# Low halves of the weights: a negated copy on ScalarE and an adding DMA instead of a VectorE subtraction

## The chip, the cores and the metric

One core of one Trainium2 chip runs the whole program. The metric is the device time of one execution in microseconds, as the median of the runs. What a measurement of this kernel can tell from no change is about 0.2%, some 3.5 us.

## The reference, cut to what matters

A two-layer trunk over L = 528 positions (16 learned meta tokens and 512 frames) of width 2048, in float32:

```
h = rms_norm(x); q, k, v, gate = split(h @ a_w_in, 4)          # 2048 x 8192
o = diff_attention(rope(q), rope(k), v)                        # 8 heads, two softmaxes each
x = x + (rms_norm(o, subln) * 0.8 * silu(gate)) @ a_w_out      # 2048 x 2048
k_sh, v_sh = split(rms_norm(x) @ w_kv, 2)                      # 2048 x 512
q, gate = split(rms_norm(x) @ b_w_in, 2)                       # 2048 x 4096
x = x + (window_attention(rope(q), k_sh, v_sh, sinks) * silu(gate)) @ b_w_out
return rms_norm(x)[:, 16:]
```

Nearly all of the arithmetic is in the five weight products, 132 tiles of 128 output features in all.

## The kernel before, in words

Everything is kept transposed: features on the 128 partitions, tokens along the free dimension. TensorE multiplies in a reduced float32 form (F32R), so each operand is split in two: a high half that is the value rounded to that form, and a low half that is the rest. A product is then three matrix products: high by high, high by low, low by high.

`proj(m, hi, lo, cols)` makes the feature tile m: 16 k tiles, three products each, over 528 tokens in two column groups of 264 (FULL, layer A and the shared K/V) or over 512 tokens in one group (REAL, layer B). It asks `wunit(m, half)` twice for a unit of weights, eight k tiles or 128 x 1024 words (512 KB). So a FULL unit is 48 matmuls and a REAL unit 24, and `proj` uses a unit's low half first in the third product of its first k tile.

`wunit` is where the change is. For each unit SyncE (SP) issues the load of the raw words (L98), ScalarE (ACT) copies them into the high half `whi` (L99), and VectorE (DVE) subtracts the high half from the raw words into the low half `wlo` (L100):

```
nc.sync.dma_start(raw[:, c], w[m, half, :, c])
act.activation(hi[:, c], raw[:, c], AF.Copy)
dve.tensor_tensor(out=lo[:, c], in0=raw[:, c], in1=f(hi[:, c]), op=ALU.subtract)
```

There are two places for raw words and three each for `whi` and `wlo`, so the preparing of a unit begins when TensorE has done with the unit three before it. The last four units of the kernel go to places of their own (`place`, the tiles `wu`), and the first two feature tiles are loaded between the pieces of x. That leaves 132 x 2 = 264 units, of which 260 use the three rotating places.

The framework's scheduler orders each engine's instructions when the program is built; what `wunit` issues is put in with raised priority. At run time each engine, and each queue that issues DMAs, takes its instructions strictly in that order. Attention is written as generators whose steps `proj` takes between its k tiles (`advance`).

The stages, in order: the six feature tiles of each of 8 heads with the attention of the head before (until about 670 us), 16 gate tiles (to 870, beside the last head's attention until 740), the output product of layer A with residual, h1 store and sums of squares (870 to 1058), the shared K/V (to 1106), 32 tiles of queries and gates of layer B with its attention (to 1540), the output product of layer B (to 1707), and the last norm.

GpSimd (POOL) has few tasks before: the turned quarter of the rope product (L298, L596), the gated product of layer A (L499), the running sums of squares (L164) and a part of the last norm (L832). It issues no DMA. `norm_b` (L549 and `rms`, L174) waits for the last sum of squares and puts four matmuls into the K/V product.

Of the kernel before, what the change touches and what calls it, by code (L numbers as in the profile page):

```python
# [10 lines left out]
AF = mybir.ActivationFunctionType  # L11
ALU = mybir.AluOpType
# [5 lines left out]
L = SEQ + META  # L18
# [9 lines left out]


class Quads:  # L30
    """Places for [128, 4, 528] words; a freed place is given out again oldest first."""

    def __init__(self, pool, prefix, n):
        self.pool, self.idle, self.n = pool, [f"{prefix}{i}" for i in range(n)], 0
# [9 lines left out]
def trunk(tc, xT, w, vecs, sinks, rope, ident_in, out):  # L44
# [18 lines left out]
    def f(ap):  # L63
        return ap.bitcast(F32)

# [1 line left out]
    ident = cst.tile([128, 128], F32, name="ident")  # L67
    vec = cst.tile([128, 70], F32, name="vec")
    snk = cst.tile([128, 16], F32, name="snk")
# [9 lines left out]
    lam = cst.tile([128, 1], F32, name="lam")  # L79
    subg = cst.tile([128, 2], F32, name="subg")  # L80

# [1 line left out]
    ready = {}  # L83

    def wunit(m, half, place=None, pieces=1, urgent=True):
        """hi and lo of eight k tiles of the weights of feature tile m."""
        if (m, half) in ready:
            return ready.pop((m, half))
        with tc.high_priority() if urgent else ExitStack():
            raw = wp.tile([128, 1024], F32, tag="raw", name="raw", bufs=2)  # L90
            if place is None:
                hi = wp.tile([128, 1024], F32R, tag="whi", name="whi")
                lo = wp.tile([128, 1024], F32R, tag="wlo", name="wlo")
            else:
                hi, lo = place[:, 0, :], place[:, 1, :]
            for i in range(pieces):
                c = slice(1024 // pieces * i, 1024 // pieces * (i + 1))
                nc.sync.dma_start(raw[:, c], w[m, half, :, c])  # L98
                act.activation(hi[:, c], raw[:, c], AF.Copy)  # L99
                dve.tensor_tensor(out=lo[:, c], in0=raw[:, c], in1=f(hi[:, c]), op=ALU.subtract)  # L100
        return hi, lo

    def advance():
        """One step of the work that waits its turn between the halves of a projection."""
        while steps:
            try:
                next(steps[0])
                return True
            except StopIteration:
                steps.popleft()  # L110
        return False
# [32 lines left out]
        return tp.tile([128, L], F32, tag="t", name=name)[:, 0:n]  # L144

    def split4(src, g, hi, lo):
        """hi + lo = src * g, exactly."""
        act.activation(hi, src, AF.Copy, scale=g)
        dve.scalar_tensor_tensor(out=lo, in0=src, scalar=g, in1=f(hi), op0=ALU.mult, op1=ALU.subtract)  # L149

# [13 lines left out]
                pl.tensor_tensor(out=self.acc[i], in0=self.acc[i], in1=t, op=ALU.add)  # L164

    def rms(parts, dst, spare):
        """dst = 1 / sqrt(mean + eps), the same in every partition; parts add up to the sums of squares."""
        n = dst.shape[1]
        ss = psS.tile([128, 2, 512], F32, tag="S", name="ss")
        k = 2 if n > 512 else 1  # L170
        step = n // k
        for s in range(k):
            for i, p in enumerate(parts):
                pe.matmul(  # L174
                    ss[:, s, 0:step], lhsT=ones, rhs=p[:, s * step : s * step + step], start=(i == 0), stop=(i == len(parts) - 1)
                )
        v = (lambda x: two(x)) if k == 2 else (lambda x: x)
        sv = ss[:, :, 0:step] if k == 2 else ss[:, 0, 0:step]
        act.activation(v(dst), sv, AF.Sqrt, bias=epst, scale=1.0 / D)
        dve.reciprocal(out=dst, in_=dst)  # L180
        a, b = spare
        dve.tensor_scalar(out=v(a), in0=sv, scalar1=1.0 / D, scalar2=EPS, op0=ALU.mult, op1=ALU.add)
        dve.tensor_tensor(out=b, in0=dst, in1=dst, op=ALU.mult)
        dve.scalar_tensor_tensor(out=a, in0=a, scalar=-0.5, in1=b, op0=ALU.mult, op1=ALU.mult)
        dve.scalar_tensor_tensor(out=dst, in0=a, scalar=1.5, in1=dst, op0=ALU.add, op1=ALU.mult)
# [13 lines left out]

    sq2 = pool("sq2", 1)  # L200

    # ================= layer A =================
    pA = ExitStack()
    ap = pA.enter_context(tc.tile_pool(name="ap", bufs=1))

# [14 lines left out]
        if q4 % 2 == 1:  # L220
            pl.tensor_tensor(out=xq[q4 - 1], in0=xq[q4 - 1], in1=xq[q4], op=ALU.add)

    # x and the first two feature tiles' weights in the order in which the products take them
    def x_in(*kts):
        for kt in kts:
            nc.sync.dma_start(xq[kt // 4][:, kt % 4, :], xT[kt])
# [25 lines left out]
        Y.free(*xqt)  # L252
        yield

    # lambda, and the gain of the heads' norm with its factors
    lp = sm.tile([128, 2], F32, name="lp", bufs=1)
    dve.tensor_tensor(out=lp[:, 0:1], in0=vec[:, G_LAM : G_LAM + 1], in1=vec[:, G_LAM + 1 : G_LAM + 2], op=ALU.mult)
    dve.tensor_tensor(out=lp[:, 1:2], in0=vec[:, G_LAM + 2 : G_LAM + 3], in1=vec[:, G_LAM + 3 : G_LAM + 4], op=ALU.mult)
# [62 lines left out]
        yield  # L321

    def scores(S, qh, ql, m, q0, n, nsplit):
        """S = q k^T for 128 rows from q0 and n keys."""
        step = n // nsplit
        for s in range(nsplit):
            k0 = s * step
            o = S[:, s, 0:step] if nsplit > 1 else S[:, m, 0:n]
            ks = slice(k0, k0 + step)
            qs = slice(q0, q0 + 128)  # L330
            pe.matmul(o, lhsT=qh[:, m, qs], rhs=qh[:, 2 + m, ks], start=True, stop=False)  # L331
            pe.matmul(o, lhsT=qh[:, m, qs], rhs=ql[:, 2 + m, ks], start=False, stop=False)  # L332
            pe.matmul(o, lhsT=ql[:, m, qs], rhs=qh[:, 2 + m, ks], start=False, stop=True)  # L333

    def combine(p, s, n):
        """p[0] = p[0] / s[0] - lambda p[1] / s[1]"""
        dve.reciprocal(out=s, in_=s)
        dve.tensor_tensor(out=s[:, 1:2], in0=s[:, 1:2], in1=lam[0:n], op=ALU.mult)
        dve.tensor_scalar(out=p[1], in0=p[1], scalar1=s[:, 1:2], scalar2=None, op0=ALU.mult)
        dve.scalar_tensor_tensor(out=p[0], in0=p[0], scalar=s[:, 0:1], in1=p[1], op0=ALU.mult, op1=ALU.subtract)  # L340

    def heads_attend(h, qh, ql, vq, vmh, qktags, vtag):
# [23 lines left out]
        def srows(i):  # L366
            n, q0 = META + 128 * (i + 1), META + 128 * i
            p = [ap.tile([128, L], F32, tag=f"p{m}", name=f"p{m}", bufs=2 - m)[:, 0:n] for m in range(2)]
            nm = sm.tile([128, 2], F32, tag="nm", name="nm")
            s = sm.tile([128, 2], F32, tag="s", name="s")  # L370
            if i < 3:
                S = psS.tile([128, 2, 512], F32, tag="S", name="S")
                for m in range(2):
                    scores(S, qh, ql, m, q0, n, 1)
                # the first chunk's rows see nothing of the second chunk's keys
                dve.memset(S[0:64, :, n - 64 : n], NEG)
                dve.tensor_reduce(out=nm, in_=S[:, :, 0:n], axis=AX.X, op=ALU.max, negate=True)
                for m in range(2):
                    act.activation(p[m], S[:, m, 0:n], AF.Exp, bias=nm[:, m : m + 1], accum_out=s[:, m : m + 1])
            else:  # L380
                for m in range(2):
                    S = psS.tile([128, 2, 512], F32, tag="S", name="S")
                    scores(S, qh, ql, m, q0, n, 2)
                    dve.memset(S[0:64, 1, HALF - 64 : HALF], NEG)
                    dve.tensor_reduce(out=nm[:, m : m + 1], in_=S[:, :, 0:HALF], axis=AX.XY, op=ALU.max, negate=True)
                    act.activation(two(p[m]), S[:, :, 0:HALF], AF.Exp, bias=nm[:, m : m + 1], accum_out=s[:, m : m + 1])
                    if m == 0:
                        yield
            combine(p, s, 128)
            wt[i] = p[0]  # L390
# [62 lines left out]
        tmeta(1)  # L453
        yield
        pv(1)
        # norm over the head's 256 features
        sq = [sq2.tile([128, L], F32, tag=t, name=t) for t in ("sq", "ss1")]
        for dt in range(2):
            act.activation(sq[dt], o[:, dt, :], AF.Square)
# [23 lines left out]
        steps.append(heads_attend(h, *args))  # L483

    def gate_tile(acc, r, o, scale, n, dst=None):
        """o = 2 scale silu(gate) o, or dst = 2 scale silu(gate)"""
        z, th = tmp("z", n), tmp("th", n)
        av = acc[:, :, 0:HALF] if n == L else acc[:, 0, :]
        v = two if n == L else (lambda x: x)
# [9 lines left out]
            pl.tensor_tensor(out=o, in0=z, in1=o, op=ALU.mult)  # L499

    def split_quad(src, P, name, n):
        """hi and lo of a place of four tiles, each in a place of its own."""
        a, ta = P.get([128, 4, L], F32R, f"{name}h")
        b, tb = P.get([128, 4, L], F32R, f"{name}l")
        for k in range(4):
# [30 lines left out]
    drain()  # L536
    pA.close()

    # ================= layer B =================
    pB = ExitStack()  # L540
    bp = pB.enter_context(tc.tile_pool(name="bp", bufs=1))
    swap = [(j + 8) % 16 if j < 16 else j for j in range(32)]
# [162 lines left out]
    held, done, at = {}, [0], [0]  # L705

    def gate_b(m):
        """The gate's product with o in o's place; held back where o is still to come."""
        g = m // 4
        acc = proj(T_GATE_B + m, hh, hl, REAL)  # L710
        if done[0] > g:
# [42 lines left out]
    m = 0  # L754
# [29 lines left out]
    for m in range(KT - LAST):  # L784
# [5 lines left out]
        act.activation(dst, dst, AF.Copy, scale=vec[:, G_F + m : G_F + m + 1])  # L790
        if m == 1:
            act.activation(warm, ss.acc[0][:, 0:1], AF.Sqrt)
    # the last tiles one half of the tokens after the other, so that the first half's end overlaps
    units, rest = [], []
    for i in range(2 * LAST):
        m, half = KT - LAST + i // 2, i % 2
# [42 lines left out]


def _rope_table(rot, period, n_rows):
    """cos and signed sin, [2, 128, L]: rows below rot of every period rows turn, the others stay."""
    inv = np.float32(THETA) ** (-np.arange(0, rot, 2, dtype=np.float32) / np.float32(rot))
    ang = np.arange(L, dtype=np.float32)[None, :] * inv[:, None].astype(np.float32)
    c, s = np.cos(ang).astype(np.float32), np.sin(ang).astype(np.float32)
# [6 lines left out]


def _tiles(wm, cols):
    """Weight columns in tiles of 128: [tile, half, 128, 8 * 128]."""
    t = wm.reshape(2, 8, 128, -1, 128).transpose(3, 0, 2, 1, 4)
    return t[cols].reshape(len(cols), 2, 128, 1024)

# [39 lines left out]
```

## Time and profile before

| | |
|---|---|
| Median of 3 runs | 1748.77 us (1748.36 to 1749.06) |
| Span of the profiled execution, first to last instruction | 1746.9 us |
| TensorE (PE) busy | 1723.8 us, 99% |
| VectorE (DVE) busy | 978.9 us, 56% |
| ScalarE (ACT) busy | 685.8 us, 39% |
| GpSimd (POOL) busy | 170.3 us, 10% |
| DMA | 167.02 MB, mean 96 GB/s |

The profile gives the profiled execution by its span; the median stands 1.9 us above it, for what lies around the first and last instruction. Busy times are those of instructions that compute; those that issue DMAs or wait are not counted. Matmuls are pipelined, so the duration of one (0.29 us for 264 columns) is longer than the distance from one to the next (0.12 us).

### The profile page before, as it was taken

To read this page: it belongs to the slowest core of one execution; us is meant where nothing else is said; L and a number is where in the kernel's file an instruction comes from. 1 tells how busy PE (TensorE), PEld (TensorE's weight loads), DVE (VectorE), ACT (ScalarE), POOL (GpSimd) and SP (SyncE) were. 2 spreads that over 40 slices of the span, in tenths; PEclk is the share of its full clock that TensorE was granted. 3 is DMA by queue.
4 is the path that set the end of the run, shared out by engine and by line. 5 is a ranking of instruction groups with operands and counts; after the bars stand their busy time and mean duration, and the time that the engine had idled before them with its cause. 6 is when DMAs were issued, how large, how long until landed. Compare 5 with 4: busy or idle time off the path is not lost.

```text
span 1746.9 us, 28756 instructions
## 1 busy us (share of the span) xinstructions
PE 1723.8 (99%) x12078; PEld 1608.9 (92%) x12078; DVE 978.9 (56%) x1533; ACT 685.8 (39%) x1261; POOL 170.3 (10%) x106
## 2 busy tenths in 40 slices
PE   8999999999999999999999999999999999999996
PEld 7999999999999999999999999888888788888886
DVE  7755555565656565543333337567677877662234
ACT  6333333343333343433223234344445554553331
POOL 2110101010101010011101110011010100001111
PEclk9999999999999999999999999999999999999998
DMA  6222222222222222222343434422222222233342
GB/s 211 97 80 78 73 73 77 81 74 84 74 74 73 86 73 76 71 93 90 97 148 134 145 129 154 133 85 73 73 72 85 72 73 73 69 110 118 121 127 97
DMA packets 55185, 167.02 MB, mean 96 GB/s; under 512 B 6032, under 2 KB 10256, under 8 KB 55056
## 3 DMA queue, kind: packets, MB, share of 16 engines
q1 hardware_dynamic: 43728, 146.04, 25.6%
q10 hardware_dynamic: 11328, 19.14, 3.3%
q8 instruction: 95, 1.56, 0.4%
q14 instruction: 34, 0.28, 0.1%
HBM read 156.64 MB, written 8.52 MB: 95 GB/s over the span
## 4 chain that ended last, share of the span: by engine, by line
PE 93%; DVE 2%; ACT 1%; POOL 0%; issue 0%; DVEq 0%; ACTq 0%; POOLq 0%
PE acc L126 81%; PE po L424 2%; PE poB L694 2%; PE TB L198 1%; PE acct L813 1%; PE SB L646 1%; PE SB L645 1%; PE S L331 1%; PE S L333 1%; PE S L332 1%; PE T L198 1%; PE Tv L198 0%; DVE wlo L100 0%; PE po L425 0%; DVE h L832 0%; PE Tm L198 0%
## 5 line engine op out<-in xcount | busy, mean ns | idle before, releaser
L99 ACT ACTIVATE whi<-raw 128x1024 fp32r<-128x1024 f32 (+1 forms) x262 | 276.1, 1054 | 620.3 <-PE acc L126 555.2
L100 DVE TENSOR_TENSOR wlo<-raw,whi 128x1024 fp32r<-128x1024 f32 (+1 forms) x262 | 325.9, 1244 | 244.7 <-ACT whi L99 239.2
L126 PE MATMUL acc<-xh,whi 128*128 128x264 f32 x2048 | 424.2, 288 | 3.5 <-ACT whi L99 2.1
L126 PE MATMUL acc<-xl,whi 128*128 128x264 f32 x2048 | 418.7, 286 | 2.2 <-DVE xl L149 2.2
L126 PE MATMUL acc<-xh,wlo 128*128 128x264 f32 x2048 | 417.7, 285 | 0.0
L126 PEld LDWEIGHTS acc<-xh,whi 128*128 128x128 f32 x2048 | 318.9, 189 | 5.4 <-ACT whi L99 2.2
L126 PEld LDWEIGHTS acc<-xl,whi 128*128 128x128 f32 x2048 | 318.6, 189 | 3.0 <-DVE xl L149 3.0
L126 PEld LDWEIGHTS acc<-xh,wlo 128*128 128x128 f32 x2048 | 317.8, 189 | 0.0
L126 PE MATMUL acc<-hl,whi 128*128 128x512 f32 x512 | 202.5, 395 | 0.0
L126 PE MATMUL acc<-hh,whi 128*128 128x512 f32 x512 | 202.4, 395 | 0.0
L126 PE MATMUL acc<-hh,wlo 128*128 128x512 f32 x512 | 201.5, 393 | 0.0
L126 PEld LDWEIGHTS acc<-hh,wlo 128*128 128x128 f32 x512 | 96.3, 188 | 22.1
L126 PEld LDWEIGHTS acc<-hh,whi 128*128 128x128 f32 x512 | 96.3, 188 | 21.8 <-DVE kt L575 0.2
L126 PEld LDWEIGHTS acc<-hl,whi 128*128 128x128 f32 x512 | 96.2, 188 | 21.0
L298 POOL TENSOR_TENSOR rr<-rr,SR 32x528 f32<-32x528 f32 x32 | 60.5, 1891 | 545.7 <-DVE rr L297 304.0
L164 POOL TENSOR_TENSOR ss<-ss,sq 128x528 f32<-128x528 f32 (+1 forms) x26 | 41.4, 1591 | 446.5 <-ACT sq L163 446.5
L657 ACT ACTIVATE p<-SB,nm 128x208 f32<-128x208 f32 (+2 forms) x128 | 51.5, 413 | 77.9 <-DVE es L654 62.4
L596 POOL TENSOR_TENSOR qr<-qr,SR 128x512 f32<-128x512 f32 x16 | 29.8, 1861 | 318.8 <-DVE qr L595 223.5
L490 DVE TENSOR_TENSOR z<-acc,rstd 128x528 f32<-128x528 f32 (+1 forms) x32 | 22.3, 698 | 59.3 <-PE acc L126 59.3
L295 DVE TENSOR_TENSOR rt<-acc,CR 128x528 f32<-128x528 f32 x30 | 21.2, 706 | 53.5 <-PE acc L126 53.5
L531 DVE TENSOR_TENSOR xr<-acc,xr 128x528 f32<-128x528 f32 x16 | 11.3, 708 | 60.1 <-PE acc L126 60.1
L300 ACT ACTIVATE qh<-rt 128x528 fp32r<-128x528 f32 x32 | 20.6, 645 | 60.0 <-DVE rt L299 60.0
(293 smaller groups left out, 2819.4 us busy)
## 6 DMA issues: line engine op xcount, KB each, us to landing
raw<-in_w SPq DMA_DIRECT2D x262, 512.0 KB, 3.3
hr<-h_dram ACTq DMA_DIRECT2D x32, 256.0 KB, 3.0
xq<-in_xT SPq DMA_DIRECT2D x16, 264.0 KB, 5.6
xr<-in_xT ACTq DMA_DIRECT2D x16, 264.0 KB, 3.6
h_dram<-xr ACTq DMA_DIRECT2D x16, 264.0 KB, 2.0
out<-h SPq DMA_DIRECT2D x4, 512.0 KB, 3.1
out<-h ACTq DMA_DIRECT2D x4, 512.0 KB, 3.9
raw<-in_w SPq DMA_DIRECT2D x4, 256.0 KB, 4.6
```

The costliest lines, as they stand in the source:

```text
L99: act.activation(hi[:, c], raw[:, c], AF.Copy)
L100: dve.tensor_tensor(out=lo[:, c], in0=raw[:, c], in1=f(hi[:, c]), op=ALU.subtract)
L126: pe.matmul(acc[:, s, 0:n], lhsT=a[:, ws], rhs=b[kt // 4][:, kt % 4, c0 : c0 + n], start=(kt == 0 and ps == 0), stop=(kt == KT - 1 and ps ...
L164: pl.tensor_tensor(out=self.acc[i], in0=self.acc[i], in1=t, op=ALU.add)
L198: pe.transpose(o, i, ident[0 : i.shape[0], 0 : i.shape[0]])
L295: dve.tensor_tensor(out=two(t), in0=acc, in1=two(CR), op=ALU.mult)
L298: pl.tensor_tensor(out=r[0:32], in0=r[0:32], in1=SR[0:32], op=ALU.mult)
L424: pe.matmul(pov[:, dt, c0:256], lhsT=v_, rhs=w_[:, j, c0:256], start=(j == 0 and k == 0), stop=False)
L490: dve.tensor_tensor(out=v(z), in0=av, in1=v(r), op=ALU.mult)
L596: pl.tensor_tensor(out=r, in0=r, in1=SR[:, META:], op=ALU.mult)
L657: act.activation(p[:, rt, 0:W], Sv[:, rt, :], AF.Exp, bias=nm[:, rt : rt + 1], accum_out=s[:, rt : rt + 1])
L694: pe.matmul(po, lhsT=vw[w_][0:k, c, g % 2, :], rhs=pp, start=(i == 0), stop=(i == len(parts) - 1))
```

## The change

For the feature tiles from 6 on, in the rotating places, the low half is no longer made by VectorE. ScalarE reads the raw words a second time and writes their negated copy, rounded to F32R, into the low half's place; then GpSimd issues a DMA that reads the same raw words from HBM again and adds them to what stands in that place. The first six feature tiles and the last four units keep the subtraction. That makes 248 units by DMA (260 less 12). The rest of the diff takes out comments and docstrings.

```
+            by_dma = place is None and m >= 6
             for i in range(pieces):
                 c = slice(1024 // pieces * i, 1024 // pieces * (i + 1))
                 nc.sync.dma_start(raw[:, c], w[m, half, :, c])
                 act.activation(hi[:, c], raw[:, c], AF.Copy)
-                dve.tensor_tensor(out=lo[:, c], in0=raw[:, c], in1=f(hi[:, c]), op=ALU.subtract)
+                if by_dma:
+                    act.activation(lo[:, c], raw[:, c], AF.Copy, scale=-1.0)
+                    pl.dma_start(lo[:, c], w[m, half, :, c], accum_op=ALU.add)
+                else:
+                    dve.tensor_tensor(out=lo[:, c], in0=raw[:, c], in1=f(hi[:, c]), op=ALU.subtract)
```

## Rows read from the trace of the kernel before

**Rows 1.** The page's first part: busy time, share of the span, instructions of each engine.
```profile
PE 1723.8 (99%) x12078; PEld 1608.9 (92%) x12078; DVE 978.9 (56%) x1533; ACT 685.8 (39%) x1261; POOL 170.3 (10%) x106
```

**Rows 2.** Busy time by stage: stretch, length, PE, PEld, DVE, ACT, POOL, PEclk, DMA share, GB/s.
```profile
90.00:740.00 650.00, 650.00 (x5411) 645.52 (x5410) 370.41 (x622) 247.95 (x469) 59.18 (x32) 1.00 0.24 77
740.00:870.00 130.00, 130.00 (x1065) 130.00 (x1064) 55.15 (x59) 40.03 (x48) 15.03 (x11) 1.00 0.28 90
870.00:1058.00 188.00, 188.00 (x1538) 188.00 (x1538) 62.77 (x67) 54.56 (x65) 20.53 (x14) 1.00 0.42 141
1060.00:1106.00 46.00, 45.92 (x373) 45.58 (x372) 35.78 (x50) 22.15 (x32) 1.88 (x1) 1.00 0.54 173
1160.00:1350.00 190.00, 190.00 (x947) 157.29 (x946) 141.29 (x257) 95.88 (x233) 14.63 (x8) 1.00 0.24 78
1350.00:1395.00 45.00, 43.90 (x228) 35.99 (x227) 35.44 (x69) 23.75 (x61) 4.44 (x3) 1.00 0.18 59
1540.00:1700.00 160.00, 160.00 (x692) 129.70 (x691) 58.67 (x66) 58.98 (x74) 18.98 (x11) 1.00 0.39 122
1700.00:1746.90 46.90, 33.73 (x241) 31.49 (x239) 20.66 (x33) 7.07 (x13) 8.39 (x9) 0.88 0.28 100
```

**Rows 3.** The chain that ended last, in order of time: start, us, what.
```profile
740.68 317.15 PE acc L126 x2592
...
1540.77 166.83 PE acc L126 x720
```

**Rows 4.** Groups of instructions: busy us, mean ns, then idle before and its releasers.
```profile
L100 DVE TENSOR_TENSOR wlo<-raw,whi 128x1024 fp32r<-128x1024 f32 (+1 forms) x262 | 325.9, 1244 | 244.7 <-ACT whi L99 239.2
...
L99 ACT ACTIVATE whi<-raw 128x1024 fp32r<-128x1024 f32 (+1 forms) x262 | 276.1, 1054 | 620.3 <-PE acc L126 555.2 <-issue 54.7 <-DMA raw<-in_w 6.9
...
L298 POOL TENSOR_TENSOR rr<-rr,SR 32x528 f32<-32x528 f32 x32 | 60.5, 1891 | 545.7 <-DVE rr L297 304.0 <-DVE s_m L337 198.4 <-DVE s_m L338 40.0
```

**Rows 5.** Who waited for whom: us in total, times, longest.
```profile
PE acc L126 <- ACT whi L99: 2.1, 1, 2.1
```

**Rows 6.** One unit of layer A's output product in order of time: start, us, instruction.
```profile
899.03 1.06 ACT L99 ACTIVATE whi<-raw 128x1024 fp32r<-128x1024 f32 x1 [3.24 <-PE acc L126]
...
900.12 1.23 DVE L100 TENSOR_TENSOR wlo<-raw,whi 128x1024 fp32r<-128x1024 f32 x1 [3.97 <-ACT whi L99]
...
911.30 0.41 PE L126 MATMUL acc<-og11h,wlo 128*128 128x264 f32 x2
```

**Rows 7.** One unit of layer B's output product in order of time.
```profile
1590.64 1.06 ACT L99 ACTIVATE whi<-raw 128x1024 fp32r<-128x1024 f32 x1 [3.21 <-PE acc L126]
...
1602.26 0.39 PE L126 MATMUL acc<-pg2h,wlo 128*128 128x512 f32 x1
```

**Rows 8.** One unit among the heads in order of time.
```profile
406.79 1.06 ACT L99 ACTIVATE whi<-raw 128x1024 fp32r<-128x1024 f32 x1 [2.38 <-PE acc L126]
...
420.04 0.41 PE L126 MATMUL acc<-xh,wlo 128*128 128x264 f32 x2
```

**Rows 9.** The loads of raw words: issue durations in ns (min/median/max), and time to landing.
```profile
L98 SPq DMA_DIRECT2D raw<-in_w x266: 327/328/432, 1.7 to 1698.8; - x133
...
DMA to landing us min/median/max: 3.1/3.3/5.8
```

**Rows 10.** DMA queues by the page: packets, MB, share of 16 engines over the span.
```profile
q1 hardware_dynamic: 43728, 146.04, 25.6%
```

**Rows 11.** The chain that ended last, from 1058 to 1066 us.
```profile
1058.92 0.94 ACT whi L99
...
1061.08 1.89 POOL ss L164
...
1063.76 1.16 PE ss L174 x4
```

**Rows 12.** The chain that ended last, from 1352 to 1396 us.
```profile
1363.14 2.35 DVE wlo L100
...
1368.61 1.23 DVE wlo L100
...
1389.95 1.23 DVE wlo L100
```

## The prediction

> **What bounds the kernel now.** I read the busy times first [rows 1]: TensorE is busy for 1723.8 of 1746.9 us, so 23.1 us are all that any change off TensorE can win back. The view by stage says where these lie [rows 2]: 13.2 us behind 1700 us, where the last four units (their low halves stay with VectorE) and the last norm end; 1.1 us at 1350 to 1395; 0.1 us in the K/V product; none in the other stages shown. What is left, 8.7 us, is before 90 us, where the first tiles (also unchanged) wait for x. So only some 1.2 us of idle TensorE lies where the change acts. The chain of waits agrees: through layer A's gate and output products it is one piece of 2592 matmuls in 317.15 us, through layer B's output product one of 720 in 166.83 us [rows 3]. That gives 5.87 us for a FULL unit of 48 and 5.56 us for a REAL unit of 24. The pace doesn't hang on VectorE: busy 57% among the heads and 33% in layer A's output product, with TensorE full in both [rows 2]. After its start TensorE waits for no weights; the one wait in the list of waits is 2.1 us at its first matmul [rows 5].
>
> Units are prepared far ahead. In layer A's output product ScalarE ends a high half at 900.09, VectorE ends the low half at 901.35, and TensorE first reads that low half at 911.30 [rows 6]: 9.9 us later. From the end of the high half there are 11.2 us; 10.6 us in layer B's output product [rows 7], 12.2 us in the tightest of the heads' units [rows 8].
>
> **The change part by part.**
>
> *VectorE loses 248 subtractions* at 1.23 us, the time of the full-sized one [rows 6], 305 us in all. Its 979 us become 674. None of this lies on the path outside 1350 to 1395, where three subtractions (2.35, 1.23, 1.23 us) stand in the chain [rows 12]. They can give back no more than the 1.1 us that TensorE idles there: -1.1, between 0 (the new ScalarE copies take their places) and -1.1.
>
> *ScalarE gains 248 negated copies.* Same shape and types as the high half's copy, so 1.06 us each, 263 us: 686 becomes 949 us, 54% of the span. The engine idles 620 us ahead of its high halves alone [rows 4], so this is cover enough, but a ScalarE task queued behind a unit comes 1.06 us later. That shows once on the path: the K/V product waits at 1063.76 for the sum of squares, in a chain that runs through a high half at 1058.92 and GpSimd's L164 at 1061.08 [rows 11], and TensorE loses only 0.1 us there now. The copy makes it +1.1 (0 if it is ordered behind the squaring).
>
> *GpSimd gains 248 DMA issues.* No row shows an issue on this engine. An issue on SP takes 0.33 us, the mean L298 takes 1.89 us [rows 9, 4]; these are the ends, and I take 1 us, as its descriptors are a program's work. GpSimd comes to 418 us, 24%. One such issue ahead of L164 in the chain of [rows 11] adds +1 (0.3 to 1.9). Otherwise L298 and its like are late by one issue, which nothing on TensorE waits for at once.
>
> *SP's loads.* A raw place is freed by the negated copy, 1.06 us behind the high half, and not by VectorE, 1.26 us behind it: nothing changes, except that the next raw load starts in the same moment as the adding DMA.
>
> *The new wait: TensorE for the adding DMA.* From the end of the high half: 1.06 us copy, then D from the copy's end to the landing. The room for D is 10.1 us in layer A's gate and output products, 9.5 us in layer B's output product, 11.1 us in the heads. No DMA of this kind is in the trace. A raw load of the same bytes lands 3.3 us after issue, the slowest after 5.8 us [rows 9]. The ends are one plain load (3.3) and two of the slowest in a row (11.6, read and then written back); I take two median ones, 6.6 us, because the place must be read as well as written but on no crowded queue. Then at least 2.9 us are left and the cost is nothing.
>
> *What the DMA engines can carry.* The SP queue's packets took 25.6% of the span for 146.04 MB [rows 10], so 0.524 MB of raw words take 1.6 us of all 16 engines. Each unit's stage already uses, per unit: gates 0.28 x 5.87 = 1.6 us; layer A's output 0.42 x 5.87 = 2.5; K/V 0.54 x 5.9 = 3.2; layer B's output 0.39 x 5.56 = 2.2 [rows 2]. What is left for an adding DMA is 4.2, 3.4, 2.7 and 3.4 us; the heads and layer B's attention, with nearly 7 us a unit, have over 5. An adding DMA takes X: the low end is one plain transfer, 1.6; the high end three, 4.8. A plain transfer is a read and a write, about 0.8 each if alike, and this one has two reads and a write: I take 2.4 us. It fits everywhere, in K/V just so.
>
> The Trainium skill speaks against this value. Its page "Collectives: The Full Stack" (Part 3, the bandwidth ceiling) says that an addition in the DMA engine runs at half the rate of a copy because both source reads go through one ring. No row here shows an addition; by that rule X would be 3.2 us, the first rival below. The page "DMA: Bandwidth & Descriptors" (Issuing engines are not separate DMA queues) adds that a DMA issued from GpSimd shares the same 16 engines, which is why X is added to the other queues' shares.
>
> *Sum.* -1.1 + 1.1 + 1 + 0 (wait) + 0 (DMA engines) = +1.0 us on the span of 1746.9: 1747.9. The median of the runs lies 1.9 us above the span, so 1749.8 us, against 1748.77. A difference under 0.2% (3.5 us) can't be told from none.
>
> **The rivals.**
>
> *Two reads at full price (X = 3.2).* For it: nothing in the rows excludes it. Only K/V is overrun, by 0.47 us in each of 8 units, 3.8 us; layer A's output (3.4) and layer B's (3.4) just hold. 1749.8 + 3.8 = 1753.6 us.
>
> *The DMA engines become the bound (X = 4.0, between 3.2 and the high end).* It decides from X = 3.4 on, in the pure products: layer A's output 0.6 x 32 units = 19 us, K/V 1.3 x 8 = 10, layer B's output 0.6 x 28 = 17: +46, 1796 us. With X = 4.8 the gates join (0.6 x 22) and it is +113. For it: the word-by-word addition is unlike anything in the trace, and these stages have the highest DMA shares. Against it: the loads' average share is now 25.6%.
>
> *The latency is too long (D = 11.6).* It decides from D = 9.5. A place is used by every third unit, so an excess is paid once in three: (11.6 - 10.1) / 3 x 62 units of gates, layer A's output and K/V = 31, (11.6 - 9.5) / 3 x 28 = 20: +51, 1801 us. Against it: the slowest plain load in the run takes half of that.
>
> *GpSimd's order.* An adding DMA queued behind L298, which waited for VectorE's shuffle for 304 us in all [rows 4], would come late; behind it in turn a rope product would stall VectorE. With D = 6.6 it needs more than 3 us at a place; with 1 us beyond that at each of 48 places, 32 heads' and 16 queries' tiles, it is +48, 1798 us. Against it: VectorE, for which GpSimd waits, loses a third of its work.
>
> *Faster.* For more than 3.5 us there would have to be waits hidden under the matmuls' modelled durations, which overlap. Against it stands the same 5.87 us in stages with busy and idle VectorE. If so, about 1744 us.
>
> *It does less than it says.* Were most units to keep the subtraction, the time would be 1748.8; the condition leaves out 16 of 264 only, so this is folded into no change.
>
> **How the numbers follow.** No change, 50%: 1749.8 us, its own range 1747 to 1752. Two reads at full price 12%, DMA engines 18%, latency 9%, GpSimd's order 7%: together slower 46%. Faster 4%. The likeliest is no change, so the time is 1749.8. The low end is 1746, below which lies only the faster case. The high end takes in latency and GpSimd's order as priced, and DMA engines up to X = 4.2 (0.8 x 32 + 1.5 x 8 + 0.8 x 28 = 60, 1809 us); beyond are about 13 in 100.
>
> **What would show it.** Right: TensorE's idle time still near 24 us and no wait of TensorE for the low half's DMA in the list; VectorE near 674 us, ScalarE near 949; a new GpSimd queue with 130 MB (248 x 0.524), its median landing under 9 us, and 34% of the 16 engines (248 x 2.4 of 1747). Wrong by the engines: DMA shares of 0.9 or more in the output products, raw loads landing late too, TensorE waiting there and not among the heads. Wrong by latency: landings above 9.5 us with shares well under 1. Wrong by order: TensorE's waits behind GpSimd tasks among the heads. The forecast is wrong if the median leaves 1745.3 to 1752.3.

## The result, and the profile after

The changed kernel takes 1769.67 us (median of four, 1763.72 to 1775.14) against 1748.91 us: ratio 1.0118, interval 1.009 to 1.0146. That is slower, by 20.8 us. The likeliest case of the prediction, no change, did not come; its rivals on the DMA engines did, in part. The profiled execution is the longest of the four, with a span of 1773.4 us against 1746.9, so its 26.5 us show what is lost a little too large.

Busy times of the kernel after:

```profile
PE 1731.8 (98%) x12078; PEld 1614.2 (91%) x12078; DVE 680.2 (38%) x1285; ACT 913.9 (52%) x1509; POOL 352.4 (20%) x354
```

VectorE did lose its subtractions, and it bought nothing. TensorE's idle time went from 23.1 to 41.6 us, and its busy time rose by 8.0 us for the same 12078 matmuls. The view by stage (columns as in [rows 2]) says where:

```profile
740.00:870.00 130.00, 130.00 (x1065) 130.00 (x1064) 29.10 (x37) 60.57 (x69) 34.11 (x33) 1.00 0.82 174
870.00:1058.00 188.00, 188.00 (x1539) 188.00 (x1538) 24.27 (x33) 82.85 (x96) 46.92 (x46) 1.00 0.95 229
1060.00:1106.00 46.00, 40.26 (x309) 39.54 (x308) 24.14 (x39) 23.97 (x29) 6.60 (x7) 0.93 0.85 207
1106.00:1160.00 54.00, 45.90 (x228) 38.84 (x228) 12.43 (x20) 23.68 (x35) 9.46 (x10) 0.91 0.73 172
1540.00:1700.00 160.00, 159.85 (x702) 129.67 (x702) 32.86 (x57) 87.24 (x118) 36.38 (x37) 1.00 0.89 205
```

Layer A's output product runs with the DMA engines 0.95 busy and TensorE full; the K/V stage behind it loses 5.7 us of 46 and the start of layer B 8.1 of 54, with a granted clock of 0.93 and 0.91 where it was 1.00. (Before, TensorE was busy all 54 us from 1106 to 1160.) By TensorE's milestones the program is 1.7 us late at the end of the heads' attention (740.68 became 742.33), 2.1 at the norm's matmuls in K/V (1063.76, now 1065.86), 17.6 at the first matmul of layer B (1106.81, now 1124.38), 20.0 from 1183 on and 26.1 at the last tiles (1707.60, now 1733.71). So some 18 of 26 us are lost between 1066 and 1183, and 6 in layer B's output product.

The DMA queues (packets, MB, share of 16 engines), to be read beside [rows 10]; then DMA issues with KB and median us to landing, beside [rows 9]:

```profile
q0 software_dynamic: 35712, 130.04, 44.7%
q1 hardware_dynamic: 43728, 146.04, 26.9%
```

```profile
raw<-in_w SPq DMA_DIRECT2D x262, 512.0 KB, 3.9
wlo<-in_w POOLq DMA_DIRECT2D x248, 512.0 KB, 7.6
hr<-h_dram ACTq DMA_DIRECT2D x32, 256.0 KB, 6.1
```

The adding DMAs carry fewer bytes than the SP queue and take far more of the engines: 44.7% of 1773.4 us over 248 is 3.20 us each. The h1 loads `hr`, 3.0 us to landing before, take 6.1; this is the median of all 32. For those of K/V alone, before and then after:

```profile
DMA to landing us min/median/max: 2.7/3.4/4.6
DMA to landing us min/median/max: 4.6/7.3/12.0
```

TensorE's waits that [rows 5] had not:

```profile
PE acc L131 <- DMA wlo<-in_w: 9.6, 3, 5.2
PE acc L131 <- DVE kt L580: 8.1, 1, 8.1
```

The chain that ended last runs through these h1 loads (start, us, what):

```profile
1081.41 9.74 DMA hr<-h_dram
...
1091.80 1.04 ACT whi L100
1092.84 0.95 ACT wlo L102
1093.79 1.23 ACT hh L153 x2
...
1095.42 6.96 DMA hr<-h_dram
...
1110.21 11.97 DMA hr<-h_dram
...
1122.20 0.73 ACT hh L153
```

Sixteen such loads, 256 KB each, pass through four places (shared with the stage's other temporary tiles) that come free only when ScalarE and VectorE have split the load before. And the split stands in ScalarE's queue ahead of the weights. In the order of time of ScalarE, then of GpSimd:

```profile
1089.08 0.73 ACT L153 ACTIVATE hh<-hr,vec 128x512 fp32r<-128x512 f32 x1 [8.52 <-DMA hr<-h_dram]
```

```profile
1094.19 0.88 POOL L103 DMA_DIRECT2D wlo<-in_w  x1 [12.37 <-ACT wlo L102]
```

ScalarE stands 8.5 us at a split whose load is late. The high half and the negated copy behind it are then late, GpSimd gets its next adding DMA after 12.4 us, and TensorE stands 5.2 us at the low half that it brings, at 1102. At the first matmul of layer B it stands 8.1 us, until VectorE has taken over the last K/V product (`kt`), a task that stands in VectorE's queue behind the last split:

```profile
1122.95 0.75 DVE L154 SCALAR_TENSOR_TENSOR hl<-hr,vec,hh 128x512 fp32r<-128x512 f32 x1 [2.34 <-ACT hh L153]
1123.62 0.70 DVE L580 TENSOR_TENSOR kt<-acc,rstd 128x528 f32<-128x528 f32 x1
```

The wait in layer B's output product, 3.9 us at 1726.80, comes the same way. In the kernel before, ScalarE made the high half of the last unit in the rotating places and then the first of the four in places of their own (`wu`):

```profile
1690.72 1.06 ACT L99 ACTIVATE whi<-raw 128x1024 fp32r<-128x1024 f32 x1 [3.15 <-PE acc L126]
1691.77 1.06 ACT L99 ACTIVATE wu<-raw 128x1024 fp32r<-128x1024 f32 x1
```

In the kernel after, the copy for `wu` stands first in ScalarE's queue, and it waits for its raw words, which take 7.9 us to land:

```profile
1715.49 1.06 ACT L100 ACTIVATE wu<-raw 128x1024 fp32r<-128x1024 f32 x1 [6.64 <-DMA raw<-in_w]
```

The chain through it (start, us, what):

```profile
1707.60 7.87 DMA raw<-in_w
1716.46 1.04 ACT whi L100
1717.50 0.96 ACT wlo L102
1718.87 7.90 DMA wlo<-in_w
1726.80 6.91 PE acc L131 x22
```

So the adding DMA lands inside the 9.5 us that the prediction left it there; it is issued late.

### The profile page after: what moved, and what is told of

Read it like the earlier page. It is cut to its first block, busy times and chain, and to the rows that moved or that the text cites. A ratio compares the mean times of both kernels' runs of the same rounds, so it can differ in the third digit from the quotient of the medians.

```text
span 1773.4 us, 29220 instructions
## 1 busy us (share of the span) xinstructions
PE 1731.8 (98%) x12078; PEld 1614.2 (91%) x12078; DVE 680.2 (38%) x1285; ACT 913.9 (52%) x1509; POOL 352.4 (20%) x354
## 3 DMA queue, kind: packets, MB, share of 16 engines
q0 software_dynamic: 35712, 130.04, 44.7%
## 4 chain that ended last, share of the span: by engine, by line
PE 84%; DMA 5%; issue 3%; DVE 2%; ACT 2%; POOL 0%; DVEq 0%; ACTq 0%; POOLq 0%
PE acc L131 73%; DMA hr<-h_dram 3%; PE po L429 2%; DMA wlo<-in_w 1%; PE poB L699 1%; PE TB L203 1%; PE acct L818 1%; PE SB L651 1%; PE SB L650 1%; PE S L336 1%; PE S L338 1%; PE S L337 1%; PE T L203 1%; ACT wlo L102 0%; DMA raw<-in_w 0%
## 5 line engine op out<-in xcount | busy, mean ns | idle before, releaser
L103 POOL DMA_DIRECT2D wlo<-in_w x248 | 216.2, 872 | 1086.6 <-ACT wlo L102 980.7
L102 ACT ACTIVATE wlo<-raw 128x1024 fp32r<-128x1024 f32 x248 | 259.0, 1044 | 0.0
L131 PEld LDWEIGHTS acc<-hh,wlo 128*128 128x128 f32 x512 | 96.9, 189 | 22.3
L131 PEld LDWEIGHTS acc<-hl,whi 128*128 128x128 f32 x512 | 96.9, 189 | 21.2
L303 POOL TENSOR_TENSOR rr<-rr,SR 32x528 f32<-32x528 f32 x32 | 43.4, 1356 | 177.2 <-DVE rr L302 173.9
L793 DVE TENSOR_TENSOR h<-acc,hr 128x512 f32<-128x512 f32 x14 | 9.7, 692 | 124.0 <-PE acc L131 124.0
L495 DVE TENSOR_TENSOR z<-acc,rstd 128x528 f32<-128x528 f32 (+1 forms) x32 | 22.3, 698 | 83.8 <-PE acc L131 83.8
L300 DVE TENSOR_TENSOR rt<-acc,CR 128x528 f32<-128x528 f32 x30 | 21.2, 706 | 72.6 <-PE acc L131 72.6
L705 DVE TENSOR_TENSOR oB<-poB,up 64x256 f32<-64x256 f32 x64 | 26.7, 417 | 44.1 <-ACT up L701 43.6
```

What stands on the lines that cost most here:

```text
L102: act.activation(lo[:, c], raw[:, c], AF.Copy, scale=-1.0)
L103: pl.dma_start(lo[:, c], w[m, half, :, c], accum_op=ALU.add)
L131: pe.matmul(acc[:, s, 0:n], lhsT=a[:, ws], rhs=b[kt // 4][:, kt % 4, c0 : c0 + n], start=(kt == 0 and ps == 0), stop=(kt == KT - 1 and ps ...
L300: dve.tensor_tensor(out=two(t), in0=acc, in1=two(CR), op=ALU.mult)
L303: pl.tensor_tensor(out=r[0:32], in0=r[0:32], in1=SR[0:32], op=ALU.mult)
L495: dve.tensor_tensor(out=v(z), in0=av, in1=v(r), op=ALU.mult)
```

## The experiments

All times are medians; "before" is the kernel before on the same chip, 1749.1 to 1749.4 us. The theory (A): an adding DMA takes twice as much of the 16 DMA engines as a plain one, which overruns the K/V stage and touches the two output products.

**Where it is lost.** The weights prepared during K/V go back to the subtraction.

```
-            by_dma = place is None and m >= 6
+            by_dma = place is None and m >= 6 and not 80 <= m < 86
```

> Tiles 80 to 85, the weights prepared during the K/V product, go back to the subtraction (12 of 248 units); all else as changed. Theory A (the adding DMAs crowd the 16 DMA engines where the h1 loads need them, so these land late and TensorE stalls in K/V and at the start of layer B): some 18 to 20 us of the loss go, about 1754 us, granted clock full in that stage, h1 loads of K/V landing in 3 to 4 us. Rival B (ScalarE's second copy delays the h1 halves, in its queue): the same loss goes here too, so this run only says where. Rival C (a small loss at every unit): at most 1 us comes back, about 1768 us.

1754.88 us, ratio 1.0031 (1.0018 to 1.0044): 14.8 us come back from 12 of 248 units, less than the 18 to 20 expected. K/V has TensorE full again:

```profile
1058.00:1106.00 48.00, 47.79 (x389) 47.45 (x389) 35.78 (x51) 23.18 (x32) 1.88 (x1) 1.00 0.51 167
```

A loss spread over all units is refuted. Of the time left over, 5.6 us, the trace shows most as one wait at the end of layer B's output product (1708.17):

```profile
PE acc L131 <- DMA wlo<-in_w: 4.0, 1, 4.0
```

**ScalarE's copies without the DMA.**

```
                     act.activation(lo[:, c], raw[:, c], AF.Copy, scale=-1.0)
-                    pl.dma_start(lo[:, c], w[m, half, :, c], accum_op=ALU.add)
+                    dve.tensor_tensor(out=lo[:, c], in0=raw[:, c], in1=f(hi[:, c]), op=ALU.subtract)
```

> ScalarE still writes the negated copy of all 248 units, but VectorE then writes the low half by the subtraction over it, and there is no adding DMA. Theory A: the loss is the DMA's, so 1749 to 1751 us. Rival B (ScalarE's copies are the loss): 1764 to 1772 us, with late h1 halves in K/V while the h1 loads land in about 3 us.

1753.5 us, ratio 1.0023 (1.0014 to 1.0032): over what the theory expected and far under the rival. Its loss is of another kind:

```profile
PE TB L203 <- DVE p L669: 4.2, 6, 1.1
```

TensorE waits for VectorE in layer B's attention: there VectorE keeps the subtraction and gets it 1.04 us later, which would explain the wait. So this run loads both engines and doesn't weigh the copy alone; the next one does.

**The same DMA without the addition.** The low halves are then the raw words.

```
-                    pl.dma_start(lo[:, c], w[m, half, :, c], accum_op=ALU.add)
+                    pl.dma_start(lo[:, c], w[m, half, :, c])
```

> GpSimd's DMA copies the raw words over the negated copy and does not add; the addition is the part left out. Instructions, waits and bytes read from HBM are as in the changed kernel. Theory A with the addition's second read as the price: the GpSimd queue's share falls from 45% to 22 to 25% of the engines, landing from 7.6 to 4 to 5 us, and the time to 1750 to 1754 us. If any second load of the same bytes is enough to crowd the engines: share and landing fall less, 1760 us or more.

1750.14 us, ratio 1.0004 (0.9994 to 1.0013). Queue shares and landing:

```profile
q1 hardware_dynamic: 43728, 146.04, 24.5%
q0 software_dynamic: 35712, 130.04, 22.3%
```

```profile
wlo<-in_w POOLq DMA_DIRECT2D x248, 512.0 KB, 4.8
```

22.3% of 1748.3 us over 248 is 1.57 us each: the addition doubles the time in the engines (3.20) and adds 2.8 us to the landing. With all copies, issues, waits and HBM bytes kept, the loss is gone. (Engine time and landing fall together here; this run doesn't part them.) ScalarE as the cause is refuted, and so is the mere second reading of the weights.

**Which read costs.** The addend comes from the place in SBUF.

```
-                    pl.dma_start(lo[:, c], w[m, half, :, c], accum_op=ALU.add)
+                    pl.dma_start(lo[:, c], raw[:, c], accum_op=ALU.add)
```

> The adding DMA takes the raw words from their place in SBUF, not from HBM; the place is freed only when it has landed. If the price is two reads and a write through the engines: still about 3.2 us a unit (43 to 46% share). If it is the second HBM read: share about 25 to 35%. The time says little here, as the next raw load now waits for the landing; 1760 to 1850 us.

One run, 1828.9 us, in the range, as the raw places come free late: TensorE waits 40.3 us for the adding DMAs. The share lies between the two cases, so neither was met:

```profile
q0 software_dynamic: 35712, 130.04, 37.4%
```

37.4% of 1827.1 us over 248 is 2.76 us, against 1.57 for a copy from HBM. Without a second read of HBM the addition still costs 1.2 us more than that copy; 0.44 us hang on where the addend lies. No run copies from SBUF without adding, so how the 2.76 us divide stays open. Landing is 5.1 us in place of 7.6.

**Half the columns.**

```
-                    act.activation(lo[:, c], raw[:, c], AF.Copy, scale=-1.0)
-                    pl.dma_start(lo[:, c], w[m, half, :, c], accum_op=ALU.add)
+                    act.activation(lo[:, 0:512], raw[:, 0:512], AF.Copy, scale=-1.0)
+                    pl.dma_start(lo[:, 0:512], w[m, half, :, 0:512], accum_op=ALU.add)
+                    dve.tensor_tensor(out=lo[:, 512:], in0=raw[:, 512:], in1=f(hi[:, 512:]), op=ALU.subtract)
```

> For all 248 units the adding DMA makes only the first 512 of 1024 columns (ScalarE negates only these), VectorE subtracts the rest. If the DMA's price goes with its bytes: 1.6 us of the engines a unit (22 to 23% share), landing 4.5 to 5.5 us, K/V not overrun, 1749 to 1752 us. If most of it is fixed per DMA or per packet: share over 30%, landing over 6 us, 1755 us or more.

1751.25 us, ratio 1.0017 (1.0007 to 1.0026).

```profile
q1 hardware_dynamic: 43728, 146.04, 30.8%
q0 software_dynamic: 35712, 65.03, 21.2%
```

21.2% of 1749.5 us over 248 is 1.50 us, near half of 3.20: the price goes with the bytes. The landing, 5.3 us, falls by less than half.

**Is it throughput or the chain of h1 loads?** Every second load of K/V gets a place of its own.

```
+    hrx, hrxt = Y.get([128, 4, L], F32, "hrx")
...
-            hr = tmp("hr", SEQ)
+            hr = tmp("hr", SEQ) if m % 2 == 0 else hrx[:, m // 2 % 4, 0:SEQ]
...
+    Y.free(hrxt)
```

> As changed, but every second h1 load of the K/V stage goes to a free place of its own (four more places, eight in all), so that more loads are under way at once. If K/V is lost to the chain load, high half, low half, place free, next load, each load late by some us: 8 to 14 us come back, 1756 to 1761 us. If the engines' throughput alone sets it: not more than 3 us come back, 1766 us or more.

1760.1 us (seven runs, 1753.72 to 1765.98), ratio 1.006 (1.0041 to 1.0078): 9.6 us come back by the medians, with the same bytes to carry. In its profile, of an execution of 1754.84 us, TensorE is busy 70.4 of 72 us from 1058 to 1130 with the engines 0.93 busy, and the `hr` loads of K/V land in 4.9 us in place of 7.3. So by the medians more than half of the K/V loss is loads late one after another, not bytes beyond what the engines carry. The runs spread as far as the gain, so the share is rough.

**Does K/V lose by itself?** Only its 12 units by DMA, then these with layer A's output product, 44 units.

```
-            by_dma = place is None and m >= 6
+            by_dma = place is None and 80 <= m < 86     # the second run: 64 <= m < 86
```

> The adding DMA only for tiles 80 to 85, the 12 units prepared during K/V; all other units keep the subtraction. Theory A in its local form (K/V is overrun by itself): 10 to 18 us of loss from these 12 units, 1759 to 1767 us. If the backlog from layer A's output product is needed: 1750 to 1754 us.

> The adding DMA for tiles 64 to 85, layer A's output product and K/V (44 units). Local form: as for the 12 units alone, plus some 3 us, 1762 to 1770 us. With backlog: clearly more than with the 12 units alone, 1763 to 1770 us against 1750 to 1754 us.

1759.88 us, ratio 1.0064 (1.0046 to 1.0081), and 1765.67 us, ratio 1.0098 (1.0072 to 1.0123). Twelve units lose 10.5 us alone; with the 32 before them it is 16.3. K/V of the first, where the engines reach 0.91, and the start of layer B behind it:

```profile
1058.00:1106.00 48.00, 46.08 (x370) 45.33 (x369) 25.69 (x41) 27.61 (x36) 7.44 (x8) 1.00 0.91 223
1106.00:1130.00 24.00, 18.14 (x86) 15.11 (x86) 5.38 (x8) 11.28 (x17) 2.61 (x3) 0.86 0.73 180
```

The local form holds: the 12 units alone fall into its range, and no backlog is needed. The 32 units before them add 5.8 us where 3 were expected; the two intervals overlap, so that a crowded stage ahead makes it worse is likely, but not shown.

**The rest.** Layer B's output product by subtraction; that with K/V and tiles 6 to 11 too; that with layer A's output product too.

```
-            by_dma = place is None and m >= 6
+            by_dma = place is None and 6 <= m < 116                          # first
+            by_dma = place is None and (12 <= m < 80 or 86 <= m < 116)       # second
+            by_dma = place is None and (12 <= m < 64 or 86 <= m < 116)       # third
```

> Only layer B's output product (tiles 116 and up, 28 units) goes back to the subtraction. Theory A (two stages are overrun, K/V and the end of layer B's output product, each for itself): about 6 us come back, 1762 to 1766 us, with the K/V stall as in the changed kernel. If the late end is a follow-up of the K/V stall: nothing comes back.

> Subtraction for tiles 6 to 11 (the first stall at 77 us), 80 to 85 (K/V) and 116 and up (layer B's output product); the adding DMA for the other 196 units: heads, gates, layer A's output product and layer B's attention. Theory A: nothing is overrun any more, 1748.5 to 1750 us, although layer A's output product still shows the engines over 0.9 busy. If crowded engines cost by themselves, layer A's output product still loses: 1752 us or more.

> The adding DMA only for tiles 12 to 63 and 86 to 115 (164 units: heads, gates of layer A, layer B's attention); subtraction in both output products and K/V. Theory A (the cost is where an adding DMA brings the engines to 0.9 and more): 1749 to 1750 us, 3 to 4 us under the run that kept it in layer A's output product too. If every unit costs a little: about 1752 us.

1766.78 us, 1.0109 (1.0083 to 1.0134); 1753.06 us, 1.003 (1.0017 to 1.0044); 1750.52 us, 1.0006 (0.9997 to 1.0016). The first gives back 2.9 us, less than expected and within its own spread (1761.94 to 1774.23), so its median doesn't decide on the 6 us. The traces say more: in this run's, TensorE is busy all of 1540 to 1700 and waits for no weights there, and in that of the first experiment, where K/V no longer stalls, the 4.0 us at the end of this stage stay. So that wait is the stage's own and no follow-up of K/V.

The second missed theory A's range: layer A's output product, 0.91 busy there, seems to cost by itself. Its trace has three waits for the adding DMA in that stage, 1.0 us in all, and 1.4 us at the norm's matmuls behind it; the trace of the third has neither. The third is 2.5 us faster by the medians, less than the 3 to 4 expected; the intervals just part, and 2.5 us is little against the 3.5 us that can be told. With the crowded stages out, 164 units by DMA cost nothing that can be told.

**A version that gains?** The adding DMA only beside layer B's attention, where VectorE is busiest.

```
-            by_dma = place is None and m >= 6
+            by_dma = place is None and 86 <= m < 116
```

> The adding DMA for tiles 86 to 115 alone (60 units, layer B's queries and gates beside its attention, where VectorE is busiest and the DMA engines are not). TensorE's 1.1 us of idle time at 1350 to 1395 shrink: 1748 to 1749 us, 0 to 1.1 us under the kernel before. If ScalarE's copies hold up the attention's chain: 1750 us or more.

1749.43 us against 1749.14, ratio 1.0003 (0.9994 to 1.0011): no gain. TensorE's idle time at 1350 to 1395 shrinks from 1.1 to 0.4 us, but 0.6 us appear in the stage behind it. This run also prices the adding DMA where the engines have time left, 0.60 to 0.72 busy from 1106 to 1540:

```profile
q0 software_dynamic: 8640, 31.46, 11.0%
```

11.0% of 1747.7 us over 60 is 3.20 us again, so the price doesn't come from crowding near 0.9. No kernel tried beats the one before.

## Why the prediction was wrong in its likeliest case

The measured 1769.67 us lies outside 1745.3 to 1752.3, where the prediction saw its likeliest case, and inside its range to 1809 us. None of its cases gives this time: the nearest are 1753.6 (X = 3.2) and 1796 us (X = 4.0). That the range took it in is in part luck: the DMA engines and K/V were named, but the rivals that widened the range did not come, or not at the strength they were priced at.

- *What bounds the kernel*: right. TensorE had next to nothing to win, and 248 subtractions taken from VectorE won nothing (680 us busy, forecast 674).
- *ScalarE*: 1.04 us a copy (1.06 forecast); 914 us, 35 under the forecast. As a cost nothing that can be told, shown by the plain DMA at 1750.14 us.
- *GpSimd*: 0.87 us an issue (1 forecast). Of the 1.1 us for ScalarE and 1 us for GpSimd that the sum put on the norm's matmuls in K/V, TensorE waits 0.5 us there.
- *The wait, D*: 7.6 us median, 9.9 at most, against 6.6 taken and 11.6 as the high end. The room of 10.1 us held: layer A's output product kept TensorE full. The latency rival is out, except at the first adding DMA (8.5 us, TensorE 0.5 us idle). What the sum left out is that the room begins with the high half, and that this can be late itself: at the end of layer B's output product it stood in ScalarE's queue behind a copy whose load was late (3.9 us).
- *What the DMA engines can carry*: **this is the step that failed.** X was taken as 2.4 us, from "two reads and a write" at 0.8 us each; it is 3.20 us, and in stages where the engines have time left too. So the term for the DMA engines, put at 0, is not 0. The Trainium skill's page "Collectives: The Full Stack" (Part 3, the bandwidth ceiling) has a reduce-scatter between cores at half the rate of an all-gather, because its addition needs two source reads on one ring. The factor agrees here: 3.20 against 1.57 us. The ring is not what was tested; the addend from SBUF, 2.76 us, only fits the same direction.
- *Two reads at full price*: the place was right, K/V, and the price was not. It was worked out as the engines' overrun, 3.8 us. Alone the 12 units lose 10.5 us, and taking them out of the change gives back 14.8. What that sum left out is the chain. The h1 loads are paced by their landing (3.4 before, now 7.3 us in K/V) through four places; four places more gave back 9.6 us. And ScalarE's queue hands their lateness to the weights behind them, seen in the trace of the changed kernel alone.
- *The clock*: left out too. In the stretches with the waits of 5.2 and 8.1 us and right behind them it fell:

```profile
1100.00:1110.00 10.00, 7.74 (x50) 7.74 (x51) 3.45 (x5) 6.19 (x11) 1.55 (x2) 0.70 0.87 250
1120.00:1130.00 10.00, 5.62 (x14) 4.47 (x15) 3.27 (x5) 4.42 (x9) 0.88 (x1) 0.51 0.45 99
```

  A granted clock of 0.70 and 0.51 says that for part of this the array ran at 1.2 in place of 2.4 GHz; between them, from 1110 to 1120, it reads 0.98. K/V matmuls of 285 ns at 1070 to 1080 average 331 ns at 1100 to 1110. From milestone to milestone the busy time grows by 2.2 us in K/V, 2.4 at the start of layer B and, behind the wait of 3.9 us (0.86 from 1720 to 1730), 2.0 in layer B's output product. These are 6.6 of the 8.0 us; another 1.3 lie before 742 us at a granted clock of 1.00, and why, no run shows.
- *The DMA engines become the bound* (X = 4.0): in this strength no, since X stayed at 3.2 and the output products still held, by 0.95 and 0.89 busy. By the last two runs of the group above, layer A's lost some 2.5 us all the same.
- *GpSimd's order*: no wait of TensorE goes back to it; GpSimd got faster (L298, now L303, 1.36 us for 1.89).

What stays open: how the runs of the changed kernel come to spread over 11 us where those before keep within 4; what in the addition takes the time; and how much the crowded output product of layer A adds to the loss in K/V.

## What to carry to other kernels

Price a DMA that adds at twice a copy of the same bytes in the engines, as measured here for 512 KB, and hold that against each stage's DMA share, not the mean. Where the engines were 0.85 to 0.95 busy here, the loads that lost were those with few places, and whoever stood behind them: one copy that waits for a late load holds up all that follows it in ScalarE's queue. A load's latency belongs in the sum wherever loads run through a few places in turn: four places paced by 7 us cost more here than the 3.8 us worked out for the engines' overrun. And work taken from an engine that TensorE didn't wait for gained nothing, though it was a third of that engine's time.

## What the runs showed that was not expected

- An adding DMA issued by GpSimd takes 3.20 us of 16 engines for 512 KB, a copy by the same path 1.57 us, an addition from SBUF 2.76 us. GpSimd is held 0.87 us by an adding issue and 0.55 by a copying one:

```profile
L103 POOL DMA_DIRECT2D wlo<-in_w x248 | 136.2, 549 | 1118.3 <-ACT wlo L102 999.4 <-ACT p L662 63.2 <-ACT wh L406 48.8
```

- With half the columns, the SP queue's unchanged loads took 30.8% of the engines where they take 24.5% beside plain DMAs; why, no run here shows.
- GpSimd's rope products ran 28% shorter in the changed kernel (1891 to 1356 ns). That VectorE's subtractions were gone is not the reason by itself: in the run that kept all of them on VectorE, behind ScalarE's second copy, they took 1385 ns. What is, no run here shows.
